# Low parts of the w_in tiles: an ACT negation and an accumulating DMA in place of DVE's subtraction

## The chip, the cores and the metric

One core of a Trainium2 chip runs the kernel. The metric is the device time of one execution in microseconds, as the median of several runs; a profiled execution of the same program gives the rows below. The engines are PE (matrix products; PEld is its weight loading), DVE, ACT and POOL (work on tiles) and SP, which only issues DMAs here.

## The reference

One layer of a hybrid decoder block, all in float32, with 512 tokens and 2048 channels:

```
h = rmsnorm(x) * (1 + scale1(c)) + shift1(c)
p = h @ w_in                        # 2048 x 5568: val, gate | r, k, v | three small parts
A = silu(group_norm(causal_conv31(val * sigmoid(gate))))
B = group_norm(rwkv7_scan(...)) + bonus, times a gate     # 16 heads of 64
x = x + gate1(c) * (concat[A, B] @ w_out)
h = rmsnorm(x) * (1 + scale2(c)) + shift2(c)
x = x + gate2(c) * ((silu(h @ w1) * (h @ w3)) @ w2)
out = rmsnorm(x)
```

scale, shift and gate are `silu(c) @ w_ada`, 2048 x 12288.

## The kernel before

Large products are made from a high and a low part of each factor: a tile x becomes xh, x rounded to the type fp32r, and xl = x - xh. A product is then three matmuls that add up in PSUM: wh with xh, wh with xl, wl with xh (`mm3`).

The weights come as a stream of units. A unit is 1 MB of weights in a tile `ws` (two buffers, loaded by SP's queue) and 48 matmuls in 16 steps. `stream` loads a unit ahead, and `split` turns quarter q of its tile (128 x 512) into `wh` and `wl` (five buffers each) at step 4q + 3 of the unit that runs before it. The copy into wh is ACT's (line 75), the subtraction into wl is DVE's (line 76). `fetch` asks for the next ws load at the start of each unit; the load needs a buffer whose four quarters have been split. Three sorts of units use the stream: `col_unit` (128 columns of w_in, channels on partitions, 37 of them here), `row_unit` and `block_unit` (w_out and the feed-forward weights).

Between the steps of the w_in units other work is woven in, by generators that are taken a step at a time: the convolution (line 839, `cy`), the sums of w_ada (line 878, `ada`, from tiles `wa`), and eight pairs of RWKV heads, one after another. Of a pair the following names matter. DVE makes `kn` (593), the matrix of a chunk, and a few rows later `r` (613), which PE waits for in `bk`. From kn, POOL makes `e` (678, 694) and `dg` (681 to 683), the diagonal blocks; SP sends these through DRAM (`d`, 686, and back as `lane`, 687) so that DVE can invert them in 15 steps (`tmp` 697, `xl` 700, one after another). The result goes through DRAM again, as it is (`D16d`) and turned by ACT (`T16d`, line 704 makes its `tmp`), and comes back as the two tiles `dd` (709, 710). POOL spreads them into `pi` and `a` (715), and PE multiplies a in `gg`. ACT copies that (729), and DVE adds the last product to `a` (732).

Every engine runs its instructions in one fixed order, which a scheduler decides when the program is built; SP and POOL also issue their DMAs in that order, so that an issue that waits holds all that stands behind it. POOL issues no DMA after the head of the program.

Of the kernel before, what the change touches and what calls it, by code (L numbers as in the profile page):

```python
# [8 lines left out]
F32 = mybir.dt.float32  # L9
F32R = mybir.dt.float32r  # L10
AF = mybir.ActivationFunctionType
ALU = mybir.AluOpType
# [23 lines left out]
class Block:  # L36
# [42 lines left out]
    def setup(self):  # L79
# [18 lines left out]
        # gm[p, q, i] : j = p % 64; strict (i > j) for q = 0, inclusive (i >= j) for q = 1  # L98
# [7 lines left out]
        # bd[p, q, i] = 1 where q == (p % 64) // 16 : the diagonal blocks of 16  # L106
# [8 lines left out]
        # m16[p, q, i] = 1 where q is odd and (p % 64) // 16 == q - 1  # L115
# [11 lines left out]
    def columns(self, pool, name, parts, dma):  # L127
        """parts: (dst name, dram ap of [rows, width]); loads the rows and returns what makes columns of them"""
        nc = self.nc
        rows = pool.tile([P, P], F32, name="rows", bufs=2)  # L130
        nc.gpsimd.memset(rows, 0.0)
        at, where = 0, {}
        for dst, ap in parts:
            n, w = ap.shape
            dma(out=rows[at:at + n, 0:w], in_=ap)
            where[dst] = (at, n)
            at += n

        def turn():
            pt = self.bg.tile([P, 512], F32, name="bk", bufs=1)  # L140
            nc.tensor.transpose(out=pt[:, 0:P], in_=rows, identity=self.ident)
            cols = self.const.tile([P, P], F32, name=name)
            nc.vector.tensor_copy(out=cols, in_=pt[:, 0:P])
            return {k: cols[:, a:a + n] for k, (a, n) in where.items()}
        return turn
# [14 lines left out]
    def cols_rest(self, pool):  # L160
        """starts the loads, then (at the next step) makes the columns"""
# [18 lines left out]
        # 1 - mu, 1 - k_a  # L180
# [31 lines left out]
    # A unit is 1 MB of weights and 48 products of [128 x 128] x [128 x 512] in 16 steps.  # L212
    def col_unit(self, w, col, xh, xl, done, before=None, stepped=None):
        """128 columns of x @ w, channels on partitions: done([P, T] in PSUM)"""
# [15 lines left out]
        return load, step, before  # L230
# [12 lines left out]
    def row_unit(self, w, ks, cc, xh, xl, accs, first, last, done, before=None, by_token=False):  # L243
        """x @ w for 4 blocks of 128 channels of x and 512 columns, tokens on partitions"""
# [10 lines left out]
    def block_unit(self, w, q, c0, xh, xl, accs, done, before=None, stepped=None):  # L255
        """4 blocks of 128 channels of x @ w, for a quarter of the channels of x; channels on partitions"""
# [12 lines left out]
    def stream(self, units):  # L269
        """units: an iterator of (load, step, before); yields after each step"""  # L270
# [9 lines left out]
        def split(p, q):  # L280
            h = self.w.tile([P, 512], F32R, name="wh", bufs=5)
            l = self.w.tile([P, 512], F32R, name="wl", bufs=5)
            self.split(h, l, p[1][:, q * 512:(q + 1) * 512])
            p[2].append(h)
            p[3].append(l)
# [24 lines left out]
    def slots(self):  # L310
        """high and low parts of 16 blocks of channels; a slot is taken again when its products are written"""
        self.XH = self.act.tile([P, KB, T], F32R, name="xh")
        self.XL = self.act.tile([P, KB, T], F32R, name="xl")
        self.slot, self.free = 0, KB
# [6 lines left out]
    def rstd_tokens(self, ss, out):  # L321
        """out = (ss / D + 1e-6) ** -0.5 on [P, n]"""
# [3 lines left out]
        # one step of Newton's: out * (1.5 - 0.5 * (ss / D + 1e-6) * out ** 2)  # L326
# [6 lines left out]
    def head(self):  # L333
        """x, the first two parts of w_ada, h by blocks of channels, and with each the lora columns
        and the first pair of heads: returns r, k, v of that in PSUM"""
# [7 lines left out]
        with self.tc.tile_pool(name="head", bufs=1) as hp:  # L343
# [25 lines left out]
            # silu(c), one column in 32, for products whose other 31 rows are zero  # L369
# [10 lines left out]
            # the last four blocks where the lora parts come later  # L380
# [27 lines left out]
            def mods(g):  # L408
                """scale and shift of the channels of group g, on partitions, added up over 4 or 128 of them"""
# [55 lines left out]
            def main(g, ws):  # L465
                """in 7 parts of 6 products"""
# [61 lines left out]
    def rwkv_pre(self, b, rkv):  # L528
        """all that does not need the state: decays, keys, the products within a chunk and their inverse"""
# [38 lines left out]
        # k / max(|k|, 1e-12) per head  # L568
# [7 lines left out]
        # by chunk b, k, b: head A takes (b, k), head B (k, b)  # L576
# [14 lines left out]
        # M transposed  # L591
# [7 lines left out]
        # V less its mean over the head; tokens on partitions: A has F (to come) over V, B has V over F  # L599
# [12 lines left out]
        # bonus  # L612
# [8 lines left out]
        # N transposed: B has A's, A has B's  # L621
# [8 lines left out]
        # b, k by chunk, tokens on partitions  # L630
# [8 lines left out]
        # Q[:, 0]: QB over QK of A; Q[:, 1]: QK over QB of B; transposed  # L639
# [17 lines left out]
        # U = X F: X goes into b and QB  # L657
# [10 lines left out]
    def inverse(self, M):  # L668
        """X[i, j] = (I - M)^-1, by chunk and head, from M transposed (strictly upper)."""
# [6 lines left out]
        # the diagonal blocks of 16, one to a lane  # L676
# [60 lines left out]
        # the blocks of 32 below the diagonal  # L737
# [19 lines left out]
    def rwkv_scan(self, b, FV, ar, bkT, Q, NV, pc, bv):  # L757
# [6 lines left out]
        # the sequence of chunks  # L764
# [33 lines left out]
        # group norm (Y has no mean within a head: V has none), bonus, gate  # L798
# [32 lines left out]
    def conv(self, b, u):  # L831
# [13 lines left out]
        # centred: PSUM to SBUF, so that the bank is free for the variance  # L845
# [14 lines left out]
    def ada(self, part, cc):  # L860
        """partial sums over the partitions, [P, 512]"""
# [23 lines left out]
    def ada_rows(self, part, cc, out):  # L885
        """on all partitions: into out, or in place of the partial sums"""
# [30 lines left out]
    def token_rstd(self, t):  # L917
        """from the squares of the four parts of the row"""
# [25 lines left out]
    def run(self):  # L944
# [31 lines left out]
        # products with w_in  # L976
# [21 lines left out]
        # products with w_out  # L998
# [34 lines left out]
        def rstd_rows(t, cc):  # L1033
            """with the last part of the row: rstd of its 128 tokens, on all partitions"""
# [8 lines left out]
        # the feed-forward part, 8 blocks of 128 hidden channels at a time  # L1043
# [71 lines left out]
        def finish(t, cc):  # L1115
            """the last norm: the gain by parts of a row, then the rstd of the row"""
# [24 lines left out]
# the order of the columns of w_in after the first pair of heads, and of the rows of w_out  # L1141
# [8 lines left out]
# steps of the stream from each step of a job to its next (the last stands for all that follow)  # L1150
# [10 lines left out]
class Lane:  # L1161
    """runs the jobs of a queue one after the other, in steps among those of the stream"""
# [15 lines left out]
    def finish(self, n):  # L1178
        """until n jobs are done"""
        while self.done < n:  # L1180
            next(self)
# [42 lines left out]
```

## Time and profile before

| | |
|---|---|
| median of 3 runs | 2545.56 us (2545.16 to 2546.66) |
| span of the profiled execution | 2543.8 us |
| PE busy | 2463.2 us (97%) |
| DVE busy | 1441.2 us (57%) |
| ACT busy | 901.1 us (35%) |
| POOL busy | 100.0 us (4%) |
| subtractions into wl, all | 740, 519.8 us of DVE |

The span is that of the engines' instructions; the time of a run holds a little more. A busy share is an average over stages: the head up to about 150 us, the stage of w_in to 866 us with the pairs of heads in it (the last pair ends later), then w_out and the feed-forward part. What an engine's time is worth is read from who waits for it.

### The profile page before, as it was taken

To read this page: it belongs to the slowest core of one execution; us is meant where nothing else is said; L and a number is where in the kernel's file an instruction comes from. 1 tells how busy PE (TensorE), PEld (TensorE's weight loads), DVE (VectorE), ACT (ScalarE), POOL (GpSimd) and SP (SyncE) were. 2 spreads that over 40 slices of the span, in tenths; PEclk is the share of its full clock that TensorE was granted. 3 is DMA by queue.
4 is the path that set the end of the run, shared out by engine and by line. 5 is a ranking of instruction groups with operands and counts; after the bars stand their busy time and mean duration, and the time that the engine had idled before them with its cause. 6 is when DMAs were issued, how large, how long until landed. Compare 5 with 4: busy or idle time off the path is not lost.

```text
span 2543.8 us, 35816 instructions
## 1 busy us (share of the span) xinstructions
PE 2463.2 (97%) x14344; PEld 1943.0 (76%) x14344; DVE 1441.2 (57%) x2553; ACT 901.1 (35%) x1461; POOL 100.0 (4%) x157
## 2 busy tenths in 40 slices
PE   6999899999999999999999999999999999999998
PEld 5767666776776767788888888888888888888886
DVE  5765888888988876686343443244324322342345
ACT  4354355356446442342222222222222222222323
POOL 2011110010010000000000000000000000000000
PEclk9999999999999999999999999999999999999999
DMA  9953344344444567556323333322332322233323
GB/s 339 346 164 84 105 117 123 93 125 139 108 107 137 183 207 227 191 190 219 122 91 99 99 100 99 96 88 98 100 99 100 99 90 94 99 100 100 99 98 114
DMA packets 275686, 336.32 MB, mean 132 GB/s; under 512 B 35619, under 2 KB 157713, under 8 KB 274496
## 3 DMA queue, kind: packets, MB, share of 16 engines
q1 hardware_dynamic: 274976, 333.85, 42.3%
q8 instruction: 112, 1.84, 0.3%
q14 instruction: 54, 0.44, 0.1%
q0 software_dynamic: 544, 0.19, 0.0%
HBM read 321.41 MB, written 12.58 MB: 131 GB/s over the span
## 4 chain that ended last, share of the span: by engine, by line
PE 85%; DVE 7%; DMA 4%; ACT 2%; issue 1%; POOL 1%; DVEq 0%; ACTq 0%; SPq 0%; POOLq 0%
PE row L67 60%; PE acc L67 14%; PE bk L67 5%; DMA wa<-in_w_ada_dram 3%; PE gg L67 2%; DVE cy L839 1%; DVE wl L76 1%; PE fp L67 1%; PE yy L67 1%; PE first L67 1%; DVE ada L878 1%; DVE tmp L697 0%; ACT L206 0%; DMA dd<-D16d 0%; PE bk L635 0%
## 5 line engine op out<-in xcount | busy, mean ns | idle before, releaser
L76 DVE TENSOR_TENSOR wl<-ws,wh 128x512 fp32r<-128x512 f32 x740 | 519.8, 707 | 847.6 <-ACT wh L75 805.5
L75 ACT CAST wh<-ws 128x512 fp32r<-128x512 f32 x740 | 458.7, 621 | 1288.0 <-PE row L67 1059.7
L67 PE MATMUL row<-xh,wh 128*128 128x512 f32 x1408 | 550.7, 391 | 0.0
L67 PE MATMUL row<-xh,wl 128*128 128x512 f32 x1408 | 548.2, 389 | 0.0
L67 PE MATMUL row<-xl,wh 128*128 128x512 f32 x1408 | 548.1, 389 | 0.0
L67 PE MATMUL row<-wh,hid 128*128 128x512 f32 x1408 | 434.6, 389 | 0.0
L67 PEld LDWEIGHTS row<-xl,wh 128*128 128x128 f32 x1408 | 264.4, 188 | 55.5 <-issue 1.0
L67 PEld LDWEIGHTS row<-xh,wh 128*128 128x128 f32 x1408 | 264.4, 188 | 55.0 <-issue 1.0
L67 PEld LDWEIGHTS row<-xh,wl 128*128 128x128 f32 x1408 | 264.3, 188 | 55.1
L67 PEld LDWEIGHTS row<-wh,hid 128*128 128x128 f32 x1408 | 264.3, 188 | 55.0 <-ACT hid L75 0.2
L67 PE MATMUL row<-wl,hid 128*128 128x512 f32 x704 | 274.0, 389 | 0.0
L67 PE MATMUL acc<-xh,wh 128*128 128x512 f32 x592 | 258.1, 436 | 2.8 <-ACT wh L75 2.8
L67 PE MATMUL acc<-xl,wh 128*128 128x512 f32 x592 | 241.6, 408 | 0.0
L67 PE MATMUL acc<-xh,wl 128*128 128x512 f32 x592 | 239.1, 404 | 0.0
L878 DVE SCALAR_TENSOR_TENSOR ada<-wa,sc,ada 128x512 f32<-128x512 f32 x256 | 191.7, 749 | 52.1 <-DMA wa<-in_w_ada_dram 46.8
L67 PEld LDWEIGHTS row<-wl,hid 128*128 128x128 f32 x704 | 132.2, 188 | 27.4
L67 PEld LDWEIGHTS acc<-xh,wh 128*128 128x128 f32 x592 | 111.9, 189 | 35.1 <-issue 5.1
L67 PEld LDWEIGHTS acc<-xh,wl 128*128 128x128 f32 x592 | 112.4, 190 | 26.5 <-issue 1.9
L67 PEld LDWEIGHTS acc<-xl,wh 128*128 128x128 f32 x592 | 112.5, 190 | 24.7 <-issue 5.7
L206 ACT ACT_TABLE_LOAD x85 | 109.1, 1283 | 2.3 <-PEq L1213 0.8
L839 DVE SCALAR_TENSOR_TENSOR cy<-cu,colC,cy 128x512 f32<-128x512 f32 x120 | 96.6, 805 | 1.7
L839 DVE SCALAR_TENSOR_TENSOR cy<-cu,colD,cy 128x512 f32<-128x512 f32 x120 | 89.2, 744 | 0.6
(330 smaller groups left out, 2354.7 us busy)
## 6 DMA issues: line engine op xcount, KB each, us to landing
ws<-in_w_ff_dram SPq DMA_DIRECT2D x132, 1024.0 KB, 5.2
wa<-in_w_ada_dram SPq DMA_DIRECT2D x256, 256.0 KB, 3.0
ws<-in_w_in_dram SPq DMA_DIRECT2D x37, 1024.0 KB, 5.9
wa<-in_w_ada_dram SPq DMA_DIRECT2D x32, 1024.0 KB, 11.5
ws<-in_w_out_dram SPq DMA_DIRECT2D x8, 1024.0 KB, 5.1
wa<-in_x_dram SPq DMA_DIRECT2D x4, 1024.0 KB, 6.1
x<-in_x_dram SPq DMA_DIRECT2D x4, 1024.0 KB, 10.7
out_dram<-x SPq DMA_DIRECT2D x8, 512.0 KB, 2.7
```

The source lines that it names most:

```text
L67: return self.nc.tensor.matmul(out, lhsT=lhsT, rhs=rhs, start=start, stop=stop, skip_group_check=True)
L75: self.nc.scalar.copy(out=hi, in_=x)
L76: self.nc.vector.tensor_tensor(out=lo, in0=x, in1=hi.bitcast(F32), op=ALU.subtract)
L206: self.last_fn = nc.scalar.preload_act_table_set(name).ins
L839: v.scalar_tensor_tensor(out=y, in0=u[:, t:t + T], scalar=self.tap(t, b), in1=y, op0=ALU.mult, op1=ALU.add)
L878: nc.vector.scalar_tensor_tensor(out=acc, in0=was[r], scalar=self.sc[:, r:r + 1], in1=acc, op0=ALU.mult, op1=ALU.add)
```

## The change

For the units of w_in, which `col_unit` now marks by a fourth element, the split has three parts: ACT copies x into wh as before, ACT writes minus wh into wl, and a DMA that POOL issues adds x onto wl in place, from SBUF to SBUF, 256 KB. The other units keep the subtraction. 148 splits of 740 are changed. The rest of the diff takes out comments, so that the lines behind `split` have numbers that are 6 higher after the change.

```diff
 def col_unit(self, w, col, xh, xl, done, before=None, stepped=None):
...
-        return load, step, before
+        return load, step, before, True
...
         def split(p, q):
             h = self.w.tile([P, 512], F32R, name="wh", bufs=5)
             l = self.w.tile([P, 512], F32R, name="wl", bufs=5)
-            self.split(h, l, p[1][:, q * 512:(q + 1) * 512])
+            x = p[1][:, q * 512:(q + 1) * 512]
+            if self.rowp is None and len(p[0]) > 3:
+                self.nc.scalar.copy(out=h, in_=x)
+                self.nc.scalar.activation(out=l, in_=h.bitcast(F32), func=AF.Identity, scale=-1.0)
+                self.nc.gpsimd.dma_start(out=l, in_=x, accum_op=ALU.add)
+            else:
+                self.split(h, l, x)
             p[2].append(h)
             p[3].append(l)
```

What that does to the order of the instructions is seen at three places. The waits in brackets name the engine or the DMA queue (HW: issued by SP; SW: issued by POOL) whose semaphore an instruction waits for.

DVE in the seventh pair, from kn to r, before:

```order
L593 TENSOR_TENSOR kn<-gg,gm 128x512 [waits DVE_49,PE_49]
L808 SCALAR_TENSOR_TENSOR f<-yy,colB,f 128x512 [waits Activation_49]
L76 TENSOR_TENSOR wl<-ws,wh 128x512 [waits Activation_49]
L809 SCALAR_TENSOR_TENSOR f<-f,colB,bv 128x512 [waits DVE_49]
L598 TENSOR_TENSOR k<-k,a 128x512 [waits Activation_49]
L814 TENSOR_TENSOR f<-f,bk 128x512 [waits DVE_49]
L609 TENSOR_TENSOR bk<-k,pi 128x8x64 [waits DVE_49]
L76 TENSOR_TENSOR wl<-ws,wh 128x512 [waits DMAHW2_49,PE_49,Activation_49]
L76 TENSOR_TENSOR f<-f,bv 128x512 [waits Activation_49]
L613 SCALAR_TENSOR_TENSOR r<-r,colB,k 128x512
```

and now:

```order
L599 TENSOR_TENSOR kn<-gg,gm 128x512 [waits DVE_49,PE_49]
L814 SCALAR_TENSOR_TENSOR f<-yy,colB,f 128x512 [waits Activation_49]
L815 SCALAR_TENSOR_TENSOR f<-f,colB,bv 128x512 [waits DVE_49]
L604 TENSOR_TENSOR k<-k,a 128x512 [waits Activation_49]
L820 TENSOR_TENSOR f<-f,bk 128x512 [waits DVE_49]
L615 TENSOR_TENSOR bk<-k,pi 128x8x64 [waits DVE_49]
L619 SCALAR_TENSOR_TENSOR r<-r,colB,k 128x512
```

The two subtractions into wl ahead of r are gone; kn, r and the steps between them are the same. In the 15 steps of the solve that follows, three subtractions stood between tmp and xl, and none stands there now.

SP in the seventh pair, from lane on, before:

```order
L687 DMA lane<-d_6990 64x256 [waits DMAHW7_49,DMAHW2_49]
L218 DMA ws<-in_w_in_dram 128x16x128 [waits DMAHW3_49,DVE_49]
L709 DMA D16d<-xl_6993 64x256 [waits DMAHW4_49,DVE_49]
L709 DMA T16d<-tmp_7267 64x256 [waits DMAHW5_49,Activation_49]
L710 DMA dd<-D16d 128x8x16 [waits DMAHW6_49,DMAHW4_49]
L710 DMA dd<-T16d 128x8x16 [waits DMAHW5_49]
```

and now:

```order
L693 DMA lane<-d_7109 64x256 [waits DMAHW7_49,DMAHW6_49]
L938 DMA mix<-bv 128x512 [waits DMAHW0_49,Activation_49]
L218 DMA ws<-in_w_in_dram 128x16x128 [waits DMASW7_49,DMASW6_49,DMAHW1_49,DMASW5_49,DMASW0_49]
L939 DMA mix<-f 128x512 [waits DMAHW2_49,DVE_49]
L715 DMA D16d<-xl_7112 64x256 [waits DMAHW3_49,DVE_49]
L715 DMA T16d<-tmp_7391 64x256 [waits DMAHW4_49,Activation_49]
L218 DMA ws<-in_w_in_dram 128x16x128 [waits DMASW4_49,DMASW3_49,DMAHW5_49,DMASW2_49,DMASW1_49]
L716 DMA dd<-D16d 128x8x16 [waits DMAHW3_49]
L716 DMA dd<-T16d 128x8x16 [waits DMAHW7_49,DMAHW4_49]
```

The ws load that stood between lane and D16d now stands between T16d and the two dd; the load between lane and D16d now is the one of the unit before, which stood ahead of d. A load waits for four DMAs that POOL issued (the four quarters of the unit two before it) and no more for DVE. Pairs 4 to 8 all have a ws load between D16d and the second dd now; before, none had.

SP in the second pair, from the second store to mix on, before:

```order
L933 DMA mix<-f 128x512 [waits DVE_49]
L709 DMA D16d<-xl_2250 64x256 [waits DMAHW2_49,DVE_49]
L709 DMA T16d<-tmp_2601 64x256 [waits DMAHW3_49,Activation_49]
L869 DMA wa<-in_w_ada_dram 128x512 [waits DMAHW4_49,DVE_49]
L710 DMA dd<-D16d 128x8x16 [waits DMAHW5_49,DMAHW2_49]
L710 DMA dd<-T16d 128x8x16 [waits DMAHW6_49,DMAHW3_49]
L869 DMA wa<-in_w_ada_dram 128x512 [waits DMAHW7_49,DVE_49]
L218 DMA ws<-in_w_in_dram 128x16x128 [waits DMAHW0_49,DVE_49]
```

and now:

```order
L939 DMA mix<-f 128x512 [waits DMAHW1_49,DVE_49]
L875 DMA wa<-in_w_ada_dram 128x512 [waits DMAHW4_49,DMAHW2_49,DVE_49]
L218 DMA ws<-in_w_in_dram 128x16x128 [waits DMASW7_49,DMASW6_49,DMAHW3_49,DMASW5_49,DMASW0_49]
L715 DMA D16d<-xl_2274 64x256 [waits DVE_49]
L715 DMA T16d<-tmp_2630 64x256 [waits DMAHW5_49,Activation_49]
L875 DMA wa<-in_w_ada_dram 128x512 [waits DMAHW6_49,DVE_49]
L875 DMA wa<-in_w_ada_dram 128x512 [waits DMAHW7_49,DVE_49]
L716 DMA dd<-D16d 128x8x16 [waits DMAHW4_49,DMAHW0_49]
L716 DMA dd<-T16d 128x8x16 [waits DMAHW5_49,DMAHW1_49]
```

A ws load that stood behind both dd is now ahead of D16d, and waits for four DMAs of POOL's.

On POOL the wl DMAs stand between its other instructions: in pair 2 one stands just ahead of pi whose wh copy is the third that ACT makes after tmp (704), in pairs 3 and 4 one stands between pi and a, and in pairs 1 and 2 one stands among e and dg. On ACT each negation follows its copy, or comes a few rows later.

## Rows read from the trace of the kernel before

**Rows 1.** The page's part 4: shares of the chain that ended last, by engine.
```profile
PE 85%; DVE 7%; DMA 4%; ACT 2%; issue 1%; POOL 1%; DVEq 0%; ACTq 0%; SPq 0%; POOLq 0%
```

**Rows 2.** Windows, the w_in stage: busy us (instructions), PEclk, DMA share, GB/s.
```profile
core 0 of [0], span 2543.8 us
...
150.00:936.00 786.00, 751.07 (x6554) 538.55 (x6554) 647.07 (x1219) 391.03 (x586) 78.94 (x93) 0.98 0.45 126
```

**Rows 3.** Waits of PE, 150 to 936 us: total us, times, longest us.
```profile
PE gg L67 <- POOL a L715: 10.3, 4, 5.6
...
PE bk L67 <- DVE r L613: 7.9, 6, 1.6
...
PE gg L67 <- DVE a L732: 6.2, 5, 2.0
...
PE bk L67 <- DVE ada L878: 4.5, 1, 4.5
```

**Rows 4.** Groups by line, 150 to 936 us: count, busy us, mean ns, idle.
```profile
L76 DVE TENSOR_TENSOR wl<-ws,wh 128x512 fp32r<-128x512 f32 x168 | 127.1, 759 | 7.4 <-ACT wh L75 6.0 <-ACT bkT L636 0.4
...
L75 ACT CAST wh<-ws 128x512 fp32r<-128x512 f32 x169 | 103.6, 618 | 220.5 <-PE acc L67 192.7 <-PE gg L67 18.3 <-issue 4.2
```

**Rows 5.** The chain of waits, 617 to 710 us: start, us, engine, what.
```profile
623.35 1.32 DVE wl L76
...
628.57 0.68 DVE wl L76
...
629.85 0.67 DVE r L613
...
654.76 1.10 PE gg L67 x32
...
656.54 0.68 DVE wl L76
...
662.35 0.61 DVE a L732
```

**Rows 6.** Timeline of SP's queue, 623 to 665 us: start, us of the issue.
```profile
639.75 0.38 SPq L218 DMA_DIRECT2D ws<-in_w_in_dram  x1
...
648.52 0.38 SPq L710 DMA_DIRECT2D dd<-D16d  x1
...
657.25 0.37 SPq L218 DMA_DIRECT2D ws<-in_w_in_dram  x1
```

**Rows 7.** Timeline of POOL, 636 to 656 us.
```profile
652.09 1.74 POOL L715 TENSOR_TENSOR a<-dd,bd 128x512 f32<-128x512 f32 x1
```

**Rows 8.** Timelines of ACT, DVE and PE, 148 to 158 us.
```profile
151.25 2.70 ACT L75 CAST wh<-ws 128x512 fp32r<-128x512 f32 x5
...
152.22 3.09 DVE L76 TENSOR_TENSOR wl<-ws,wh 128x512 fp32r<-128x512 f32 x5
...
153.87 1.42 PE L67 MATMUL acc<-xh,wl 128*128 128x512 f32 x1
```

**Rows 9.** DMA issues: count, KB each, median us from issue to landing.
```profile
ws<-in_w_in_dram SPq DMA_DIRECT2D x37, 1024.0 KB, 5.9
...
mix<-bv SPq DMA_DIRECT2D x7, 256.0 KB, 2.8
...
dd<-D16d SPq DMA_DIRECT2D x8, 64.0 KB, 2.8
...
rows<-in_norm_g_dram POOLq DMA_DIRECT2D x1, 8.0 KB, 5.6
```

**Rows 10.** Timelines of SP, ACT and POOL in pair 2, 284 to 302 us.
```profile
289.09 0.46 SPq L709 DMA_DIRECT2D D16d<-xl  x1
...
291.70 0.62 ACT L75 CAST wh<-ws 128x512 fp32r<-128x512 f32 x1 [1.60 <-PE acc L67]
...
294.41 0.62 ACT L75 CAST wh<-ws 128x512 fp32r<-128x512 f32 x1 [2.09 <-PE acc L67]
...
294.94 4.86 POOL L715 TENSOR_TENSOR pi<-dd,bd 128x512 f32<-128x512 f32 x1 [3.35 <-DMA dd<-D16d]
```


## The prediction

> **What bounds the kernel now.** I read the page first, then the w_in stage by windows, then the waits of PE in it, and last the chain of waits inside one pair of heads. The chain is PE for 85% of the span and DVE for 7% [rows 1]. So only a change of what PE waits for can move the time. The edited subtractions lie in the stage from 150 to 936 us, where PE is busy 751.07 of 786 us [rows 2]: whatever the change does for PE there, it cannot give more than the 35 us that are left. The waits name who holds PE: POOL's a 10.3 us in 4 waits, DVE's r 7.9 in 6, DVE's a 6.2 in 5, and one wait of 4.5 for ada [rows 3]. DVE's part is 18.6 us, so removing work from DVE is worth at most that, although 168 subtractions of 759 ns (127.1 us of DVE) stand in the stage [rows 4]. Nearly all of that DVE time lies under PE.
>
> Where wl does lie on the path is seen in the pair that begins at 617 us [rows 5]: subtractions of 1.32 and 0.68 us stand ahead of r, for which PE waits, and one of 0.68 ahead of the run that ends in a (662.35). The wl that is made there is not urgent itself: wh and wl are written about one unit of 16 steps ahead of their use. A unit's length is the distance of two ws loads, from 639.75 to 657.25, 17.5 us [rows 6].
>
> A second path runs beside PE: kn, e and dg on POOL, d and lane by DMA, the 15-step solve on DVE, D16d, T16d and the two dd by DMA, then pi and a on POOL, then PE's gg. In this pair a ends at 652.09 + 1.74 = 653.83 [rows 7] and PE starts gg at 654.76 [rows 5]: a margin of only 0.9 us. If this path gets longer by more, PE waits; if it does not get shorter, what PE gains at r is lost again at a.
>
> **What the change removes.** 148 subtractions leave DVE. Two effects reach PE.
> 1. r: the two wl rows between kn and r are gone. That is 2.0 us in the pair shown, more than a wait of 7.9 / 6 = 1.3 us [rows 3, 5]. But in the pairs with the small margin at a, PE only arrives earlier there. I count two of the six waits, -2.6 us; bounds 0 and -7.9.
> 2. DVE's a: one wl of 0.68 us less before it, in 5 waits [rows 3, 5]: -3.4 us; bounds 0 and -6.2.
> The ada wait of 4.5 us I leave as it is; it may go (bound -4.5).
>
> **What it adds.**
> 3. The start. Before, the five wh copies start at 151.25, the first wl at 152.22, and PE takes it at 153.87 [rows 8]. Now two copies and two negations alternate on ACT; the negation is one pass of ACT over the same tile as a copy, so I price it as the copy, 0.62 us [rows 4]. The first is done about 153.0. POOL then issues (0.4 us, as SP's issues of dd take [rows 6]) and the data land. No row shows an accumulating transfer. A plain one of 256 KB lands in 2.8 us (mix from bv); POOL's own queue took 5.6 us for 8 KB at the crowded beginning [rows 9]. I take 4.5, between: PE's third product comes at about 157.9 rather than 153.87, +4.0 us. Bounds +2.3 and +5.1.
>
> The Trainium skill, DMA: Bandwidth & Descriptors, section "Anatomy of one DMA — SWDGE (gpsimd) path", gives such a transfer a fixed 2.0 us plus its bytes at 436 GB/s, which for 256 KB is an estimate of 2.6 us. By that the start would cost +2.1 and the whole sum would be 1.9 us lower; POOL's rows of 5.6 us for a few KB speak against so short a time where the DMA engines are busy.
>
> 4. Later units hide the landing: negation, issue and 4.5 us make 5.5 us, and a unit of 17.5 us lies between making and use. What is not hidden is SP's queue. A ws load could go when DVE's last wl of its predecessor was done; now it waits for four landings, about 5 us later. The order shows two consequences.
>  - In pairs 4 to 8 a ws load now stands between D16d or T16d and a dd; before, it was issued at 639.75, well ahead of dd at 648.52 [rows 6]. The solve is shorter by three wl rows of about 0.7 us, -2.1; the ws issue adds 0.4; dd now goes out right behind 1 MB. A ws lands in 5.9 us, a dd alone in 2.8 [rows 9]; I add the difference, 3.1. Less the margin of 0.9 this is +0.5 us for each of five pairs, +2.4. Bounds: 0, when dd is not hindered, and +16.5, when dd waits out the whole ws (5.9 in place of 3.1, 3.3 each).
>  - In pair 2 the ws load stands ahead of D16d, which was issued at 289.09 with nothing like it in front, and a wl DMA whose copy comes after that at 294.41 stands ahead of pi, which began at 294.94 [rows 10]. The copies are 2.7 us apart there, so the awaited one is at about 297 and pi can begin at about 298.5; since pi took an unusual 4.86 us there and may now take less, I count +3.0; bounds 0 and +9.
> 5. POOL in pairs 3 and 4: a wl DMA stands between pi and a, and a waits for its negation and issue, 0.62 + 0.4, and some waiting for ACT: +1.2 each, +2.4. Bounds 0 and +8, since two wl also stand inside dg in pairs 1 and 2.
> 6. ACT: 148 negations of 0.62 us, 92 us. The cover is ACT's idle time ahead of the copies, 220.5 us, most of it waiting for PE [rows 4]. Where a negation stands just ahead of an ACT step of the chain (the copy of gg) it delays it by up to 0.62; with eight pairs at most 5 us, I take +2.
>
> **The sum.** -2.6 - 3.4 + 4.0 + 2.4 + 3.0 + 2.4 + 2.0 = +7.8 us on the profiled execution. Its span is 2543.8 us [rows 2] and some 1.8 us lie around it by the median of 2545.56. So 2543.8 + 1.8 + 7.8 = 2553.4 us, 0.3% slower.
>
> **The rivals.** A measurement of this kernel tells a difference from none at about 0.2%, 5.1 us.
> - *Balance, 2545 us.* The loads pass without hindering dd, pair 2 costs nothing because its pi is quick, and the start's +4 meets the -6 of r and a. For it: every landing has 17.5 us of cover, and the dd bound includes zero. Against it: the margin of 0.9 us at a.
> - *Faster, 2533 us.* This is the other side, and one mechanism: the path from kn to a becomes shorter than PE's work beside it. The solve loses three wl, e and f on POOL and DVE lose a neighbour, and pi comes some 2 us earlier. Then all of r (7.9), a (6.2) and part of POOL's a (10.3, of which I take 3) go, less 4 at the start: about -13. It decides as soon as dd lands less than about 2.6 us later than alone (2.1 + 0.9 - 0.4), which my 3.1 only just misses.
> - *Much slower, about 2580 us.* The accumulating transfer is slow, 10 us and more, or POOL can't issue while DVE is busy. ws loads then come late at SP, and every D16d, dd and wa behind them: +3.3 us for dd in five pairs, 9 in pair 2, 8 on POOL and up to 10 at the start, less the gains. In the rows, pi took 4.86 us in pair 2 [rows 10], where the a of the pair shown took 1.74 [rows 7], so POOL's work does stretch at times.
>
> The Trainium skill, SBUF — State Buffer, in its "DVE blocks DMA" trap, says that a POOL-issued DMA cannot get its descriptors written while DVE runs a two-port operation, with 620 ns becoming about 3100. By that rule this last rival would hold; it names fp32 copies as such operations, and the long DVE steps here read two tensors or PSUM, so no run here shows the lock on a DMA.
>
> **How the numbers follow.** My forecast (2548 to 2560) gets 0.40, of which 0.06 lies below +0.2%; balance 0.22; faster 0.24; much slower 0.14. So faster 0.24, same 0.28, slower 0.48. The range cuts half of the faster case below 2532 and half of the slow one above 2582. The bounds alone give -18.6 + 2.3 = -16 us on one side and +5.1 + 16.5 + 9 + 8 + 5 = +44 on the other, 2529 to 2589.
>
> **What the profile after would show.** Right: PE's waits for r and DVE's a nearly gone; a new PE wait of some 4 us for a DMA into wl near 154 us; waits for POOL's a larger than 10.3 us in sum; ws issued just ahead of dd in pairs 4 to 8, and dd landing in over 5 us; DVE busy some 110 us less, ACT 92 more. Wrong: wl landing so late that PE waits for it within the steady units, or dd landing in 3 us in spite of the ws ahead of it.

## The result and the profile after

The changed kernel takes 2587.53 us (median of 4 runs, 2580.74 to 2590.95) and the kernel before 2545.36 (4 runs, 2543.61 to 2546.66) in the same comparison: a ratio of 1.0161 [1.0149, 1.0174], 42.2 us slower. The forecast was 2553.4 with a range up to 2582, so the direction was right and the size was not. The profiled execution of the changed kernel has a span of 2579.0 us; it is the fastest of the four runs (2580.74), so the rows below hold 35 of the 42 us (2579.0 - 2543.8).

The page of the changed kernel, parts 1, 3 and 5 (busy time, the DMA queues with packets, MB and share of 16 engines' span, and the group of the new DMAs with its idle time):

```profile
PE 2473.7 (96%) x14344; PEld 1946.8 (75%) x14344; DVE 1351.8 (52%) x2405; ACT 983.3 (38%) x1609; POOL 221.7 (9%) x305
...
q1 hardware_dynamic: 274976, 333.85, 40.6%
q0 software_dynamic: 21856, 39.00, 9.1%
...
L287 POOL DMA_DIRECT2D wl<-ws x148 | 129.8, 926 | 409.0 <-ACT wl L286 350.8
```

DVE has given up 89.4 us of busy time and ACT has taken 82.2, where about 110 and 92 were forecast. What is new is queue q0: 39 MB that the 148 transfers move, beside the 334 MB of SP's queue. Of POOL's 409 us of idle time ahead of its issues, 350.8 are waits for ACT's negations.

The stage of the edit, by windows that end behind the last product with wl in each kernel (columns as in [rows 2]). Before:

```profile
150.00:866.50 716.50, 687.92 (x6240) 495.77 (x6242) 591.64 (x1122) 356.06 (x537) 78.81 (x92) 0.99 0.44 122
```

and after:

```profile
150.00:901.70 751.70, 699.39 (x6240) 501.33 (x6242) 503.98 (x975) 437.48 (x683) 200.57 (x238) 0.97 0.72 168
```

The stage is 35.2 us longer, which is the whole difference of the two spans. PE does the same work in it, 6240 matmuls, is 11.5 us more busy at a mean granted clock of 0.97 rather than 0.99, and stands idle 52.3 us (751.70 - 699.39) rather than 28.6. DVE's busy time fell by 87.7 us, and the stage is longer all the same. Apart from ACT's, with its negations, two columns went up: POOL's, by its 148 issues, and the DMA engines' busy share, to 0.72 from 0.44.

Who holds PE now, 140 to 1000 us in the changed kernel (as [rows 3], total us, times, longest):

```profile
PE gg L67 <- POOL a L721: 12.9, 6, 6.5
PE gg L67 <- DVE a L738: 9.7, 6, 3.1
PE fp L67 <- DVE S L794: 8.0, 3, 4.3
...
PE acc L67 <- DMA wl<-ws: 3.8, 1, 3.8
```

Of the four waits of [rows 3], those for r (7.9) and for ada (4.5) are gone. DVE's a went up from 6.2 to 9.7, POOL's a from 10.3 to 12.9, and S, which held PE for less than 1 us before, costs 8.0. The new wait for wl stands once, at the start of the stage; no later wl is late. These four are 34.4 us, where the four of [rows 3] were 28.9, so they hold only some 6 of the 23.7 us by which PE is more idle. Much of the rest is in waits that were not there or under 1 us before: for xl of the solve (3.6 and 2.5 us), for ACT's wh in `bk` (3.6 in 5 waits) and for DVE's e (2.4).

Behind PE's waits stand DVE's. The waits of DVE in the kernel before, 140 to 960 us:

```profile
DVE ada L878 <- DMA wa<-in_w_ada_dram: 9.9, 11, 2.4
...
DVE tmp L697 <- DMA lane<-d: 4.5, 2, 2.3
```

and in the changed kernel:

```profile
DVE ada L884 <- DMA wa<-in_w_ada_dram: 42.8, 28, 6.0
...
DVE tmp L703 <- DMA lane<-d: 31.5, 8, 5.4
```

DVE is less busy and waits 60 us longer for transfers that the diff doesn't touch: wa, tiles of w_ada in SP's queue, and lane, 64 KB on the path from kn to a. Not all of the 60 us comes from the transfers: in the experiments below a kernel without a DMA of POOL's waits 16.7 us for wa and 16.5 for lane in the same order (e9). The landings of the changed kernel (as [rows 9]):

```profile
ws<-in_w_in_dram SPq DMA_DIRECT2D x37, 1024.0 KB, 5.8
wl<-ws POOLq DMA_DIRECT2D x148, 256.0 KB, 4.7
...
dd<-D16d SPq DMA_DIRECT2D x8, 64.0 KB, 6.2
```

dd takes 6.2 us where it took 2.8, and ws about what it took [rows 9]. The new transfer itself lands in 4.7. The trace dates few landings of dd (of those from D16d one now, two before), but the time from the issue of dd to the start of pi on POOL says the same: in pairs 4 to 7 it was 2.3 to 3.5 us and is 6.3 to 7.0.

The chain of waits in the sixth pair of the changed kernel (counted by kn in the trace; the pair of [rows 5] is the same one):

```profile
661.29 6.97 DMA dd<-D16d
...
703.02 6.97 DMA wa<-in_w_ada_dram
...
710.55 0.48 PE fp L67 x4
```

The stretch has six transfers on it; the two longest, 6.97 us each, are shown. The first is the one forecast: the timeline of SP's queue there has

```profile
660.80 0.38 SPq L218 DMA_DIRECT2D ws<-in_w_in_dram  x1
661.29 1.48 SPq L716 DMA_DIRECT2D dd<-D16d  x1
```

with the ws load issued just ahead of dd. The second is not in the prediction at all. The timeline of DVE at that place (in brackets the idle time ahead of an instruction and its releaser):

```profile
709.43 0.75 DVE L884 SCALAR_TENSOR_TENSOR ada<-wa,sc,ada 128x512 f32<-128x512 f32 x1 [6.04 <-DMA wa<-in_w_ada_dram]
710.21 0.28 DVE L794 SCALAR_TENSOR_TENSOR S<-fp,pc,Sp 128x64 f32<-128x64 f32 x1
```

An ada step, whose sum nobody awaits there, waits 6.04 us for its late wa; S stands behind it in DVE's fixed order, and PE's fp waits for S. So a late transfer that is not urgent in itself holds PE by way of an engine's order.

### The profile page after: what moved, and what is told of

It reads as the page before. It is cut to its first block, busy times and chain, and to the rows that moved or that the text cites. A ratio compares the mean times of both kernels' runs of the same rounds, so it can differ in the third digit from the quotient of the medians.

```text
span 2579.0 us, 36204 instructions
## 1 busy us (share of the span) xinstructions
PE 2473.7 (96%) x14344; PEld 1946.8 (75%) x14344; DVE 1351.8 (52%) x2405; ACT 983.3 (38%) x1609; POOL 221.7 (9%) x305
## 4 chain that ended last, share of the span: by engine, by line
PE 71%; DVE 7%; DMA 5%; ACT 2%; issue 1%; POOL 1%; DVEq 0%; POOLq 0%; ACTq 0%
PE row L67 58%; PE acc L67 8%; DMA wa<-in_w_ada_dram 4%; DVE cy L845 2%; PE bk L67 2%; DVE ada L884 1%; PE gg L67 1%; PE fp L67 1%; DMA lane<-d 1%; DVE tmp L703 1%; ACT L206 1%; PE yy L67 1%; DVE xl L706 1%; DMA d<-dg 0%; PE row L1055 0%
## 5 line engine op out<-in xcount | busy, mean ns | idle before, releaser
L76 DVE TENSOR_TENSOR wl<-ws,wh 128x512 fp32r<-128x512 f32 x592 | 406.0, 690 | 846.7 <-ACT wh L75 805.8
L287 POOL DMA_DIRECT2D wl<-ws x148 | 129.8, 926 | 409.0 <-ACT wl L286 350.8
```

The lines of the kernel that those rows point to most:

```text
L76: self.nc.vector.tensor_tensor(out=lo, in0=x, in1=hi.bitcast(F32), op=ALU.subtract)
L287: self.nc.gpsimd.dma_start(out=l, in_=x, accum_op=ALU.add)
```

## The experiments

**Theories on record after the result.** The first theory was the forecast's own mechanism, only larger: the landings, and the ws loads that wait for them in SP's queue. Rivals: the load on the DMA engines by itself, whoever waits for a landing; the new order of all instructions, which the scheduler decides anew when DVE's rows are gone; and the negations on ACT. The runs come in four groups. Times are medians, beside the kernel before in the same comparison.

**1. Parts of the change.** Two kernels make only some quarters of a unit the new way, one has DVE add the negated copy instead of a DMA, one lets POOL subtract.

```diff
-            if self.rowp is None and len(p[0]) > 3:
+            if self.rowp is None and len(p[0]) > 3 and q == 3:     # e1 (e2: q < 3)
...
-                self.nc.gpsimd.dma_start(out=l, in_=x, accum_op=ALU.add)
+                self.nc.vector.tensor_tensor(out=l, in0=x, in1=l.bitcast(F32), op=ALU.add)      # e3
...
-                self.nc.scalar.activation(out=l, in_=h.bitcast(F32), func=AF.Identity, scale=-1.0)
-                self.nc.gpsimd.dma_start(out=l, in_=x, accum_op=ALU.add)
+                self.nc.gpsimd.tensor_tensor(out=l, in0=x, in1=h.bitcast(F32), op=ALU.subtract) # e4
```

Last quarter alone: 

> Only the last quarter of each w_in unit uses the negation and the accumulating DMA; the other three keep DVE's subtraction. Every ws load still waits for a DMA landing (that of the last quarter), but only 37 of the 148 transfers remain. Queue theory (the time is lost because a ws load waits for landings and holds dd and wa behind it on SP's queue): nearly the whole loss stays, +25 to +42 us over the kernel before. Traffic theory (148 transfers of 256 KB make all other transfers slower): a quarter of the loss, about +10 us.

First three quarters: 

> The first three quarters use the negation and the DMA, the last quarter keeps DVE's subtraction, which is what a ws load then waits for last, as in the kernel before. 111 of 148 transfers remain. Queue theory: hardly a loss, -5 to +8 us. Traffic theory: three quarters of it, about +30 us.

Negation on ACT, addition on DVE: 

> ACT copies and negates as in the change, but DVE adds x onto the tile in place of the DMA: ACT's 148 extra passes alone. If they matter by themselves: +10 us or more. Queue and traffic theory: within 5 us of the kernel before.

POOL's subtraction: 

> POOL subtracts (x minus wh into wl) in one instruction of its own: no negation, no DMA, DVE relieved as in the change. Queue and traffic theory: the loss goes, and what DVE's relief is worth is seen, -15 to +5 us; a loss here would say that work on POOL or the order that the relief of DVE brings costs time whatever the DMA does.

| | us | before | ratio |
|---|---|---|---|
| last quarter (37 DMAs) | 2560.87 | 2545.6 | 1.0060 [1.0041, 1.0078] |
| three quarters (111 DMAs) | 2586.50 | 2545.6 | 1.0162 [1.0147, 1.0177] |
| DVE adds, no DMA | 2560.27 | 2545.6 | 1.0056 [1.0041, 1.0071] |
| POOL subtracts | 2612.34 | 2545.6 | 1.0269 [1.0245, 1.0292] |

It is not only the last quarter, whose landing lets the next ws go: a quarter of the DMAs costs 15.3 us, three quarters 40.9, all 42.2. And a kernel without one DMA and with DVE's work undiminished is 14.7 us slower, so something other than transfers costs as well. POOL as the subtractor is worse than the DMA. But in these four the scheduler made a new order each time, so none of them changes one thing. The next runs hold the order fixed.

**2. The same edits with the order held.** At the program's end each engine's instructions are chained, by edges that only order them, as a table taken from another build says; instructions that the table lacks find their own place. Line numbers of such a kernel differ by one or two.

```diff
+def in_order(tc, added):
...
+        for a, b in zip(order, order[1:]):
+            tc.add_manual_dep(mine[b], mine[a].name, edge, reason="order")
```

e5 is the change in the order of before, e6 the subtraction of before in the order of after, e7 and e8 are e3 and e4 in the order of before.

The change in before's order: 

> The change, with every engine's other instructions held in the order that they have in the kernel before (PE, DVE, ACT, POOL and SP each); only the negations and the added DMAs find their own places. Order theory (the time is lost because the scheduler, with the subtractions gone, puts less urgent work ahead of what PE waits for, and moves the ws loads): the loss goes, -10 to +8 us against the kernel before. Theory of the work itself (the transfers, their landings, POOL's issues and the negations cost the time in any order): +25 us or more stay.

The subtraction in after's order: 

> The subtraction on DVE as before, with every engine's other instructions held in the order of the changed kernel. No negation, no added DMA. Order theory: most of the loss is there all the same, +25 us or more. Theory of the work itself: within 8 us of the kernel before.

Negation and DVE's addition in before's order: 

> ACT negates and DVE adds, no DMA, in the order of the kernel before. Without the order held this was +15 us. Order theory: within 6 us of the kernel before. If ACT's 92 us of negations cost time by themselves: about +15 us again.

POOL's subtraction in before's order: 

> POOL subtracts, no negation and no DMA, in the order of the kernel before. With the scheduler's own order this was +67 us. Order theory: -15 to +10 us. If POOL's work and its port shared with DVE cost the time: +40 us or more.

| | us | before | ratio |
|---|---|---|---|
| e5, change in before's order | 2617.61 | 2547.23 | 1.0279 [1.0263, 1.0294] |
| e6, subtraction in after's order | 2582.03 | 2547.23 | 1.0145 [1.0124, 1.0166] |
| e7, negation and DVE's addition | 2561.46 | 2547.23 | 1.0062 [1.0046, 1.0079] |
| e8, POOL's subtraction | 2584.52 | 2547.23 | 1.0150 [1.0134, 1.0165] |

Order is worth tens of microseconds by itself: the kernel before, with not one operation changed, loses 34.8 us when its rows stand as in the changed kernel. And the change in the old order is worse still, +70.4. There DVE's waits (140 to 1000 us) have

```profile
DVE tmp L704 <- DMA lane<-d: 62.8, 7, 13.0
```

and SP's timeline in the sixth pair shows why:

```profile
667.04 0.38 SPq L219 DMA_DIRECT2D ws<-in_w_in_dram  x1
667.51 4.39 SPq L693 DMA_DIRECT2D d<-dg  x1
```

POOL's timeline there has the last dg:

```profile
662.84 0.80 POOL L690 TENSOR_TENSOR dg<-dg,e 128x128 f32<-128x128 f32 x1
```

It is ready at 662.84 + 0.80 = 663.64 us, but d goes out at 667.51, right behind a ws load that waits for the landings of wl. So the queue mechanism of the prediction's term 4 is real. In the changed kernel's own order this load goes out behind lane (d at 643.91, lane at 646.10, ws at 647.66).

The two changes interact, then: with the added DMAs the scheduler's new order is 28.2 us better than the old one (+42.2 against +70.4), with the subtractions it is 34.8 worse. So the price of a step holds only beside the other steps as they stand there.

e7 repeats the loss of e3 (14.2 and 14.7 us), so that loss is not the order's, against the expectation of the order theory. e10 below has the negations at no such price, so it hangs on DVE's addition, which waits for ACT's negation where the subtraction waited for the copy; by what path it costs 14 us is not shown. e8 lies between its two ranges: with the order held, POOL's subtraction still costs 37.3 us, and the other 29 of e4 come with the scheduler's order.

**3. Relief, order and traffic apart.** Six kernels take the change to pieces. With the DMA left out, wl holds minus wh and not the low part; with `l = h` there is no low part and PE reads wh in its place; PE's products are as many in all of them.

```diff
-                self.nc.gpsimd.dma_start(out=l, in_=x, accum_op=ALU.add)     # e9, e10: no DMA
...
-                self.nc.scalar.activation(out=l, in_=h.bitcast(F32), func=AF.Identity, scale=-1.0)
-                self.nc.gpsimd.dma_start(out=l, in_=x, accum_op=ALU.add)
+                l = h                                                        # e11, e12
...
-                self.nc.gpsimd.dma_start(out=l, in_=x, accum_op=ALU.add)
+                self.nc.gpsimd.dma_start(out=l, in_=h.bitcast(F32), accum_op=ALU.add)      # e13
...
-                self.nc.gpsimd.dma_start(out=l, in_=x, accum_op=ALU.add)
+                self.nc.gpsimd.dma_start(out=l[:, 0:16], in_=x[:, 0:16], accum_op=ALU.add) # e14
```

Negations alone, after's order: 

> All instructions of the changed kernel in its order, negations too, but the 148 added DMAs are left out, so wl holds only minus wh (the low part of x is not added). DVE is relieved as in the change. If the DMAs cost the time (landings that a ws load waits for, transfers, POOL's issues): most of the loss goes, below +15 us. If the order and ACT's negations cost it: +30 us or more stay.

Negations alone, before's order: 

> The same work (no added DMAs, wl holds only minus wh), but the other instructions in the order of the kernel before. With the DMAs this was +70 us. If the DMAs cost the time: -15 to +12 us. If ACT's negations cost +14 us by themselves whatever DVE does: +5 to +14 us, as DVE's relief gives a part of it back.

No low parts, before's order: 

> No low parts of the w_in tiles are made at all (the products with wl read wh in their place, so PE's work is the same), in the order of the kernel before: what relieving DVE of 148 subtractions is worth by itself. By the terms of the prediction -6 to -18 us; if nothing of it lay on the path, within 4 us.

No low parts, the scheduler's own order: 

> The same work as without low parts, but in the order that the scheduler gives it by itself. If the scheduler's own order costs time when the subtractions go: 15 us or more above the same work in the order of the kernel before. If it does not: within 6 us of it.

DMA that adds wh, after's order, so that the ws load need not await it: 

> The changed kernel in its order, all 148 DMAs of 256 KB, but each adds wh in place of x (so wl becomes zero, not the low part). A ws load then waits for ACT's copies alone, not for a landing. If the waits of ws loads for landings cost the 40 us: +2 to +15 us against the kernel before. If the transfers themselves or POOL's issues cost it: +30 us or more.

DMA of 16 of 512 columns, after's order, awaited as in the change: 

> The changed kernel in its order, 148 DMAs from ws, but each adds only 16 of 512 columns (8 KB; the other columns of wl stay at minus wh). ws loads wait for landings as in the change, POOL issues as often, the traffic is gone. If the traffic costs the 40 us: +2 to +12 us. If the waits for landings or POOL's issues cost it: +25 us or more.

| | us | before | ratio | difference |
|---|---|---|---|---|
| e11, no low parts, before's order | 2526.59 | 2545.33 | 0.9928 [0.9912, 0.9944] | -18.7 |
| e10, negations alone, before's order | 2529.83 | 2545.33 | 0.9941 [0.9921, 0.9960] | -15.5 |
| e12, no low parts, own order | 2544.34 | 2545.33 | 0.9996 [0.9982, 1.0010] | -1.0 |
| e9, negations alone, after's order | 2547.93 | 2545.33 | 1.0014 [1.0000, 1.0028] | +2.6 |
| e14, small DMA, after's order | 2546.94 | 2546.61 | 1.0005 [0.9994, 1.0016] | +0.3 |
| e13, DMA from wh, after's order | 2576.02 | 2546.61 | 1.0117 [1.0090, 1.0144] | +29.4 |
| the change | 2587.53 | 2545.36 | 1.0161 [1.0149, 1.0174] | +42.2 |

Read down, the table is the change in steps:

- DVE's subtractions gone, all else in place: -18.7 us.
- Negations on ACT: +3.2 (e10 less e11), which is not to be told from nothing either.
- The scheduler's order in place of the old one: +18.1 (e9 less e10); the pair without negations gives +17.7 (e12 less e11, where the scheduler's order is another than the changed kernel's).
- 148 issues and landings with hardly any bytes: -2.3 (e14 less e9), which is not to be told from nothing.
- The bytes: +41.9 (the change less e14). Of these 29.1 come with no ws load waiting for the landings (e13 less e14), and some 12.8 from ws loads that do wait (the change less e13). e13's own interval is 7 us to either side, so this split is open by as much.

The relief and the order are each about 18 us and nearly cancel; what is left is the bytes. e10, e11 and e14 came out just beyond the ranges expected of them, e11 with a little more gain than -18.

The waits show the step from e14 to the change, in which nothing differs but the size of a transfer. The views of e14, DVE's waits (140 to 960 us) and the page's part on DMA issues and queues:

```profile
DVE tmp L704 <- DMA lane<-d: 16.6, 7, 3.5
DVE ada L885 <- DMA wa<-in_w_ada_dram: 14.7, 18, 2.4
```

```profile
q0 software_dynamic: 21856, 1.41, 1.5%
...
wl<-ws POOLq DMA_DIRECT2D x148, 8.0 KB, 2.9
```

and DVE's waits in e13:

```profile
DVE ada L885 <- DMA wa<-in_w_ada_dram: 35.4, 23, 4.7
DVE tmp L704 <- DMA lane<-d: 30.1, 8, 5.4
```

With as many packets but 1.41 MB in place of 39, DVE waits 14.7 us for wa and 16.6 for lane; with the bytes back, but no ws load waiting for them, 35.4 and 30.1, close to the 42.8 and 31.5 of the change. So it is the bytes that make other transfers late. The waits of e14 itself are no longer than those with no DMA of POOL's in the same order (e9: 16.7 and 16.5).

The order's cost shows in e9's waits of PE:

```profile
PE gg L68 <- DVE a L738: 12.8, 6, 3.1
...
PE gg L68 <- POOL a L721: 1.0, 1, 1.0
```

Without transfers the path from kn to POOL's a is short enough (1.0 us, where before has 10.3), but DVE's a costs 12.8, twice that of [rows 3]. In e14, with the small DMAs, the wait for POOL's a is

```profile
PE gg L68 <- POOL a L722: 3.7, 2, 3.0
```

and in the change it is 12.9. What stands ahead of DVE's a is seen in DVE's timeline of e9, in the sixth pair:

```profile
640.59 12.19 DVE L845 SCALAR_TENSOR_TENSOR cy<-cu,colC,cy 128x512 f32<-128x512 f32 x13
...
654.15 0.68 DVE L738 TENSOR_TENSOR a<-a,gg 128x512 f32<-128x512 f32 x1
```

and in that of e11, in the old order and also with no DMA:

```profile
636.12 11.25 DVE L845 SCALAR_TENSOR_TENSOR cy<-cu,colC,cy 128x512 f32<-128x512 f32 x12
...
648.60 0.68 DVE L738 TENSOR_TENSOR a<-a,gg 128x512 f32<-128x512 f32 x1
```

In both a long run of the convolution's steps stands ahead of a, which needs gg from PE. PE starts gg at 645.99 us in e9 and a follows 8.2 us later, and PE waits; in e11 gg starts at 642.97 and a follows 5.6 us later, and PE doesn't wait here. The run in e9 is one step longer, and it begins 5.4 us ahead of gg rather than 6.9. Why it begins later is not shown. The whole step from e10 to e9 is seen in the profiled executions too (spans of 2528.2 and 2545.1 us): of these 16.9 us PE's busy time takes 7.2 with the same 14344 matmuls, and DVE's a grows from 0.4 to 12.8, while r (3.8 to 0) and POOL's a (4.1 to 1.0) give some back.

**4. What is left to gain without the change.** If DVE's relief in the old order is worth 18.7 us because r and a come sooner, some of it should be had by moving subtractions behind r, and a two rows earlier, with no added transfer. e15 to e18 are the kernel before, in the old order but for rows of the table like these:

```diff
 TENSOR_TENSOR bk<-k,pi 128x8x64
-TENSOR_TENSOR wl<-ws,wh 128x512
 TENSOR_TENSOR f<-f,bv 128x512
 SCALAR_TENSOR_TENSOR r<-r,colB,k 128x512
+TENSOR_TENSOR wl<-ws,wh 128x512
...
+TENSOR_TENSOR a<-a,gg 128x512
 TENSOR_TENSOR wl<-ws,wh 128x512
 SCALAR_TENSOR_TENSOR cy<-cu,colD,cy 128x512
-TENSOR_TENSOR a<-a,gg 128x512
...
-DMA ws<-in_w_in_dram 128x16x128
 DMA d<-dg 128x8x16
 DMA mix<-bv 128x512
 DMA mix<-f 128x512
 DMA lane<-d 64x256
+DMA ws<-in_w_in_dram 128x16x128
```

e15 moves 11 subtractions behind r, and a; e16 also 16 more behind the solve; e17 moves the 11, and on SP the eight ws loads ahead of d behind lane; e18 is e15 with these loads moved.

> The kernel before, all its subtractions on DVE, every engine in its order, but on DVE the subtractions between kn and r stand behind r, and a stands two rows earlier. If r and a are where the relief of 18.7 us lies: -5 to -14 us. If most of it lies in the solve or elsewhere: within 4 us.

> As the run before, and the subtractions in the second half of the 15-step solve stand behind it. If the path over the solve, D16d and dd holds the other part of the relief: 3 us or more faster than the run before. If not: within 2 us of it.

> The kernel before in its order, with the subtractions between kn and r behind r, and on SP the ws load that stands ahead of d put behind lane. If that load, waiting for the moved subtractions, held d and lane: the 23 us go and part of r's 7.9 us is gained, -2 to -9 us against the kernel before. If the moved rows cost the time in another way: +15 us or more stay.

> The same, and a two rows earlier on DVE. If DVE's early wait at a is harmless: 1 to 5 us faster than the run before. If it holds what stands behind a: slower than the run before.

| | us | before | ratio |
|---|---|---|---|
| e15, r and a | 2569.30 | 2546.61 | 1.0090 [1.0076, 1.0103] |
| e16, and the solve | 2590.80 | 2546.61 | 1.0170 [1.0156, 1.0184] |
| e17, r and ws | 2542.11 | 2546.74 | 0.9985 [0.9976, 0.9994] |
| e18, r, a and ws | 2540.98 | 2546.74 | 0.9977 [0.9968, 0.9986] |

e15 did what it was meant to for r (PE's wait for it 1.8 us, where 7.9 stood) and lost 22.7 us. SP's timeline in its sixth pair:

```profile
637.30 0.38 SPq L219 DMA_DIRECT2D ws<-in_w_in_dram  x1
637.77 1.59 SPq L691 DMA_DIRECT2D d<-dg  x1
```

and its waits of DVE and PE:

```profile
DVE tmp L702 <- DMA lane<-d: 33.4, 7, 6.5
...
PE gg L68 <- POOL a L720: 20.2, 7, 4.4
```

The ws load waits for the subtractions that were moved, and d stands behind it in SP's queue: the same queue, with no added transfer. With these loads moved behind lane the wait for lane is 5.7 us, POOL's a 11.6, and the gain appears:

```profile
PE gg L68 <- POOL a L720: 11.6, 4, 5.6
...
DVE tmp L702 <- DMA lane<-d: 5.7, 4, 2.3
```

e18 is 5.8 us faster than the kernel before, the fastest version here that leaves nothing out, though by little more than can be told from no change. It and e17 are 1.1 us apart, so what moving a gives is not shown. 12.9 us of the 18.7 that the relief was worth are not had in this way.

e15 and e16 came out far from all that was expected of them. Moving the subtractions behind the solve (e16) cost another 21.5 us: PE's wait for POOL's a is 40.1 us in 8 waits there. In its sixth pair SP's ws load goes out at 665.70, behind subtractions that were moved, and D16d right after it, at 666.13, lands in 5.6 us. That is the same queue once more, one transfer further on; whether it makes up all of the 21.5 us is not shown.

## Why the prediction was wrong in size

By its own steps:

- **Term 1, r (-2.6, bound -7.9).** The wait for r is gone from the trace, as said. The nearest measure of its worth is e17, 4.6 us faster than the kernel before, where that wait falls from 7.9 to 2.0; but e17 moves ws loads as well.
- **Term 2, DVE's a (-3.4).** Wrong in sign: the waits went up by 3.5 us. The term took one wl of 0.68 us from ahead of a and left every other row where it was. Where every other row does stay (e11) the wait for DVE's a goes, so the mechanism was right for the old order. In the changed kernel's order, with the DMAs left out, the same wait is 12.8 us. That is one part of the order's cost of 18 us, for which the sum has no term.
- **Term 3, the start (+4.0).** Measured 3.8, with a landing of 4.7 us where 4.5 was estimated. The Trainium skill, DMA: Bandwidth & Descriptors, section "Anatomy of one DMA — SWDGE (gpsimd) path", gives a fixed 2.0 us plus the bytes at 436 GB/s, an estimate of 2.6 us for 256 KB. The trace has 3.3 at the least.
- **Term 4, SP's queue (+2.4 and +3.0).** The step that failed. It says that the later landings are hidden and that what is not hidden is SP's queue; hence it prices a transfer by who waits for its own landing, and for dd by the one ws ahead of it. dd did land in 6.2 us rather than 2.8. In e9, with the same ws load ahead of dd but no DMA of POOL's, it lands in 5.1, and pi starts 5.2 to 6.6 us behind the issue of dd (before 2.3 to 3.5, in the change 6.3 to 7.0): that much is the queue, about as priced. But the 148 transfers raise the DMA engines' busy share from 0.44 to 0.72 of the stage, and with that lane and wa come late: the bytes cost 29.1 us where no ws load awaits the landings and 41.9 as the change has it, where the whole term was +5.4. It is not every transfer: ws lands in 5.8 us, as before. The working has no term for a transfer's load on transfers that don't depend on it, and no bound that would have held one.
- **Term 5, POOL (+2.4).** PE's wait for POOL's a grew by 2.6 us, near the forecast, but that was luck. It is the sum of a path that is shorter without the transfers (1.0 us in e9) and of transfers that made it longer again by 11.9. The reason given, POOL's issues, is at most 2.7 of these, for with hardly any bytes the wait is 3.7 (e14); the bytes are the other 9.2.
- **Term 6, ACT (+2).** Measured +3.2 in before's order, with an interval that holds both 2 and nothing. The wait of PE for ACT's wh in `bk`, 3.6 us in 5 waits, is of that size.

The sum took its gains from rows of the old order and its losses from the new one. Relief alone was indeed worth more than forecast, -18.7 rather than -6.0. PE's waits in e11, with no low parts and in before's order:

```profile
PE gg L68 <- POOL a L721: 6.8, 3, 3.1
...
PE bk L68 <- DVE r L619: 1.6, 6, 0.4
```

The wait for r falls to 1.6 us, that for DVE's a goes, and that for POOL's a falls from 10.3 to 6.8, since that path profits too, as the rival "faster" said. In the change the order took this gain back. The rival "much slower" had nearly the right time for other reasons: the landing is 4.7 us, not 10 and more, and no POOL issue took over 1563 ns. Most of the signs that the prediction named for itself came true (r's wait gone, 3.8 us for wl at the start, more than 10.3 for POOL's a, ws issued just ahead of dd, dd landing in over 5 us) while the time did not: none of them looked at lane or wa. The views of the new DMAs in the changed kernel (least, median and longest ns of an issue; landings):

```profile
L287 POOL DMA_DIRECT2D wl<-ws x148: 860/869/1563, 151.9 to 875.6; - x148
...
DMA to landing us min/median/max: 3.3/4.7/9.0
```

The Trainium skill, SBUF — State Buffer, "DVE blocks DMA" trap, says that POOL can't write a DMA's descriptors while DVE runs a two-port operation, as its fp32 copies are. Here no issue is over 1563 ns with DVE busy 67% of the stage (503.98 of 751.70), so no run here shows that lock. The page that did bear on the case is the Trainium skill's DMA: Bandwidth & Descriptors, section "Issuing engines are not separate DMA queues": transfers of all issuing engines run on the same 16 DMA engines and interleave. e14 against the change agrees: what POOL issues delays wa and lane, which SP issues.

What stays open: why the long runs of DVE's steps begin later in the new order, and why PE's matmuls are slower in it, which together with DVE's a are what the traces show of the order's 18 us; how the bytes' 41.9 us divide between wa, lane and the ws loads; and whether another order would keep the relief and bear the traffic; e5 shows only that the old one doesn't (+85.9 us from e10 to e5, the DMAs alone).

## What to carry to other kernels

Price a transfer that is added also by its bytes: add its load to the DMA share of the stage, list the small transfers that a waiting engine needs there, and look at what stands behind each of their users in the engine's order. When work leaves an engine under a scheduler, read the new order ahead of the steps that others wait for; the gain of the relief (18.7 us here) and the cost of the order (18.1) can cancel, and the order that is worse without the transfers can be the better one with them. And a load that waits does so at the head of its queue: before moving what it waits for, look at which small transfer stands behind it.

## What the runs showed of the hardware

- An accumulating transfer of 256 KB from SBUF to SBUF lands in 4.7 us in the median, one of 8 KB with as many rows in 2.9. POOL spends 869 ns on an issue, twice what was estimated from SP's.
- POOL's subtraction of a tile takes 1461 ns in e8 where DVE's took 756 to 759, and DVE's own steps are longer beside it. The group of the convolution's first steps in e8, 150 to 960 us:

```profile
L845 DVE SCALAR_TENSOR_TENSOR cy<-cu,colC,cy 128x512 f32<-128x512 f32 x120 | 123.3, 1027 | 2.8 <-ACT cy L842 0.5
```

  Before, the same 120 take 805 ns in the mean, and 849 in e11, which has the order of e8 and no subtraction on POOL. In this case, work that POOL takes from DVE is thus paid for on DVE too.
- A small transfer that SP issues right behind a 1 MB load of ws lands late even where nothing else is added: d in 6.3 us rather than 3.1 (e15), D16d in 5.6 rather than 1.9 (e16), dd in 5.1 rather than 2.8 (e9). Its issue is longer too, 1.2 to 1.6 us in the sixth pair of e15 and e16, where the kernel before has 0.37 to 0.46.
- PE's granted clock falls behind a wait of PE. The windows of the changed kernel around the wait for S:

```profile
704.00:707.00 3.00, 2.26 (x15) 1.17 (x13) 0.00 (x0) 2.63 (x4) 0.00 (x0) 1.00 1.18 268
707.00:710.00 3.00, 0.00 (x0) 0.00 (x0) 0.57 (x1) 1.25 (x1) 0.00 (x0) 0.85 0.67 249
710.00:713.00 3.00, 2.45 (x12) 1.67 (x12) 2.92 (x8) 0.00 (x0) 0.00 (x0) 0.50 0.47 133
713.00:717.00 4.00, 4.00 (x19) 3.11 (x19) 2.28 (x4) 2.94 (x7) 0.50 (x1) 0.63 0.73 237
717.00:720.00 3.00, 3.00 (x25) 1.75 (x23) 1.80 (x5) 2.12 (x4) 0.49 (x2) 1.00 0.93 244
```

  PE stands idle from about 706 to 710.5 us. The granted clock, 1.00 (2.4 GHz) before, is then at 0.50 (1.2 GHz) while PE works again, 0.63 in the mean of the next four microseconds, and 1.00 from 717 on. So a wait costs its length and slower matmuls behind it; part of the 11.5 us by which PE's busy time in the stage grew is of this kind.
